# Another step order for four attention mixers, dearer VectorE time in the planner, a two-scalar probability scaling and a last norm that reads PSUM

## The chip, the cores and the metric

One core of one Trainium2 chip runs the whole program. The metric is the device time of one execution in microseconds. Five engines work side by side, each through its own queue in order: TensorE (PE, its weight loads shown apart as PEld), VectorE (DVE), ScalarE (ACT), GpSimd (POOL) and SyncE (SP), which issues most DMAs.

## The reference

Two decoder blocks run one after the other on one sequence of 512 tokens of width 1024, all in float32. The first block is a sparse-attention mixer (compressed, selected and windowed keys, 16 heads), a gated convolutional FFN, a sliding-window mixer with sinks, and a second such FFN. The second block is an "even" mixer (banded attention with sinks beside multi-scale pooling), a squared-ReLU MLP, an "odd" mixer (latent attention beside a bidirectional gated recurrence), and a second MLP. Cut to what matters here:

```python
h = h + mixer(rms_norm(h, g))
h = h + ffn(rms_norm(h, g2))
# inside each attention
p = exp(s - max(s)); p = p / sum(p)      # the scaling of the probabilities
o = p @ v
# at the very end
return rmsnorm(x, final_norm)            # y * rsqrt(mean(y*y) + eps) * g
```

## The kernel before

Activations lie transposed, 128 features by 512 tokens a tile. Every float32 product is made from three products of halves: both operands are split into a rounded high part and a low remainder, so that one projection of a 128-column tile over 1024 features is 24 matmuls of 512 columns. `load` (L866) fetches a weight unit of 512 KB by SP, copies it to the high half (ACT by default) and subtracts to get the low half (DVE by default).

All work is first recorded (`Recorder.add`) and then put in order by `Recorder.order`, a list planner: it walks a simulated time, and at each free engine takes the ready instruction with the lowest number that fits. `Recorder.price` gives each instruction a cost, a latency and a lock (L470 to 506). Some instructions carry alternatives: a copy may go to ACT or DVE (`copy`), a subtraction to DVE or POOL (`tt` with `spare`), a scaling of probabilities (`norm`, L821) to POOL, DVE or ACT. In `best` (L546) the engine that is free compares its wait, its latency and a tax (`TAX`, L355) times its cost with those of the others. The planner's lock rule lets a POOL instruction start at the end of the DVE instruction that holds the lock, and a DVE instruction wait for POOL's.

Within the four mixers the numbers come from hand-written words, `ORDERS` (L359): `play` (L1048) calls one step for each word. `Q`, `K`, `C`, `O` are projections, `a` one tile of scores with its softmax, `p` the transposes of four probability tiles and their product with the values, `L` the reload of one tile of the residual by DMA, `U` one eighth of half of the output projection, and the rest belongs to one mixer each (`c` compression, `G` gates, `T` `D` `E` `S` the recurrence, `P` `M` the pooling). A word's place is a priority. The FFNs and MLPs between the mixers have no words.

The last MLP is made in two halves of 256 columns. `final` (L1847) adds the result to the residual, keeps the sum of squares, multiplies by the gain on ACT, and at the end of a half `after` (L1860) makes the inverse root, spreads it over the partitions by transposes into a PSUM bank, copies that bank to SBUF and multiplies eight tiles by it, on DVE or POOL as the planner chooses, each pair followed by its output DMA. A helper records every operation, so the profile puts all of them on L723.

Of the kernel before, what the change touches and what calls it, by code (L numbers as in the profile page):

```python
# [12 lines left out]
OP = mybir.AluOpType  # L13
# [324 lines left out]
def _width(v):  # L338
# [13 lines left out]
SPILL = {("vector", "gpsimd"): 1.5, ("gpsimd", "vector"): 1.5, ("scalar", "vector"): 2.0, ("scalar", "gpsimd"): 2.0,  # L352
         ("vector", "scalar"): 1.0}
BOOST = 0
TAX = {"gpsimd": 1.0, "vector": 1.0}  # L355
MARGIN = {}
DEEP = 12
DMAQ = 2.0
HORIZON = 3000  # L359
ORDERS = {  # L360
# [26 lines left out]
}  # L387
PATIENCE = 3.0

# [3 lines left out]
class Recorder:  # L393
# [66 lines left out]
    def price(self, eng, name, args, kw, outs, ins):  # L460


        n = max([_width(v) for v in outs + ins if v.idx.size] or [1])
        if name == "dma_start":
            c = 0.48 if any(v.buf.kind == "dram" for v in ins) or not ins else 0.65
            return c, c, ""
        if eng == "tensor":
            lhs, rhs = (args[1], args[2])
            if name == "transpose":
                return 0.109, 0.109, ""  # L470
            w = _width(rhs)
            if lhs.steps and lhs.steps[-1][0] == "bitcast" or lhs.buf.dtype == F32:
                c = max(4 * w / 2400 + 0.0133, 0.214)
            elif lhs.buf.dtype == R32:
                c = max(w / 2400 + 0.0133, 0.112)
            else:
                c = max(w / 2400 + 0.003, 0.056)
            return c, c, ""
        psum = any(v.buf.kind == "bank" for v in ins)
        half = outs[0].shape[0] <= DH if outs else False  # L480
        scalars = sum(isinstance(a, View) and a.shape[1:] == (1,) for a in args[2:] + (kw.get("scalar"),))
        if eng == "scalar":
            w = _width(outs[0])
            c = w / 1200 + (0.055 if psum else 0.11) + 0.18 * isinstance(kw.get("accum_out"), View) + 0.1 * half
            return c, max(c, w / 1200 + (0.175 if psum else 0.205)), ""
        if eng == "vector":
            lock = "D" if n > 64 else ""
            if name == "reciprocal":
                return 0.07, 0.153, ""
            if psum or outs[0].buf.kind == "bank":  # L490
                c, lock = n / 960 + 0.065 + 0.1 * half, ""
            elif name in ("tensor_copy", "memset"):
                c = n / 1920 + 0.075
            elif name == "tensor_scalar":
                c = n / 1920 + 0.065 + 0.07 * scalars
            elif name == "tensor_tensor_scan":
                c = n / 480 + 0.065
            else:
                c = n / 960 + 0.075 + 0.05 * scalars + 0.09 * half
            return c, c + 0.085, lock  # L500
        if name == "tensor_scalar":
            return 0.2 + n / 1100, 0.25 + n / 1100, "p"
        if name == "memset":
            return 0.04 + n / 1100, 0.1 + n / 1100, "p"
        c = (1.0 if OP.pow in kw.values() else 0.05) + n / 445
        return c, c + 0.04, "P"


    def order(self):
# [20 lines left out]
        events, now, result = [0.0], 0.0, []  # L530
        dma_free, table, switched = 0.0, None, -99.0
        slow, window, busy, over = True, 0, 0.0, 0.0
        held = {"D": 0.0, "P": 0.0, "p": 0.0, "": 0.0}

        def arrive(op):
            heapq.heappush(wait[op.eng], (op.ready, op.n, op))
# [8 lines left out]
        def best(op, e):  # L545

            def wait(x):
                lock = cost_on(op, x)[2]
                return max(0.0, held["P"] - now) if lock == "D" else max(0.0, held["D"] - now) if lock else 0.0
            here = wait(e) + cost_on(op, e)[1] + TAX.get(e, 0.0) * cost_on(op, e)[0]  # L550
            for x in (op.eng, *op.alt):
                if x == e:
                    continue
                q = max(0.0, free_at[x] - now)
                for _, _, o in ready[x][:DEEP]:
                    if o is op:
                        break
                    if not o.done and o.eng == x:
                        q += o.cost
                there = max(q, wait(x)) + cost_on(op, x)[1] + TAX.get(x, 0.0) * cost_on(op, x)[0]  # L560
                if there + MARGIN.get((x, e), 0.0) < here:
                    return False
            return True
# [55 lines left out]
        while left:  # L619
# [7 lines left out]
            for e in engines:  # L627
# [7 lines left out]
                while i < min(len(ready[e]) - 1, 200):  # L635
# [43 lines left out]
                    at = now  # L679
                    if op.lock == "D":  # L680
                        at = max(now, now + 0.85 * (held["P"] - now))
                    elif op.lock:
                        at = max(now, held["D"])
                    held[op.lock] = at + cost
                    free_at[e] = at + cost
                    op.end = at + lat
                    if op.fn[0] == "dma_start":
# [54 lines left out]
def _body(tc, ctx, d, out):  # L742
# [76 lines left out]
        nc.vector.tensor_tensor(**kw, alt=[["gpsimd", "tensor_tensor", (), kw]] if spare else None)  # L819

    def norm(o, i, a):  # L821
        nc.gpsimd.tensor_scalar(o, i, a, None, op0=OP.mult, alt=[
            ["vector", "tensor_scalar", (o, i, a, None), {"op0": OP.mult}],
            ["scalar", "activation", (o, i, AF.Copy), {"scale": a}]])

# [106 lines left out]
        nc.gpsimd.tensor_tensor(out=r, in0=ms, in1=e, op=OP.pow)  # L932
        return r

    def spread(r):

        nb = _width(r)
        ps, rb = bank()[:, :nb * P], get()[:, :nb * P]
        for t in range(nb):
            nc.tensor.transpose(ps[:, t * P:(t + 1) * P], r[:, t:t + 1].to_broadcast([P, P]), ident)  # L940
        copy(F(rb), ps)
        return rb

    def norm_out(gains, accs, spill=None):
# [903 lines left out]
    def final(c):  # L1848
# [9 lines left out]
            act(g, hm, scale=pr("fin2")[:, m:m + 1])  # L1858

        def after():  # L1860
            rb = stats(acc)[1]
            for m in range(KT):
                g = gained[m // 2]
                tt(g[:, m % 2], g[:, m % 2], F(rb), OP.mult, True)
                if m >= KT - 2:
                    (nc.sync, nc.scalar)[m % 2].dma_start(out[:, m, c], g[:, m % 2])
                elif m % 2:
# [28 lines left out]
```

## Time and profile before

| | us |
|---|---|
| median of 3 runs | 2329.74 (2329.46 to 2330.76) |
| the profiled execution, whole | 2331.64 |
| its span, first to last instruction | 2329.5 |
| PE busy | 2257.8 (97%) |
| DVE busy | 1719.9 (74%) |
| ACT busy | 968.8 (42%) |
| POOL busy | 242.0 (10%) |
| mean granted clock of TensorE | 0.988 |

The chain of waits shows the stages. The sparse mixer's attention lies from about 75 to 328 us, its FFN to 737, the sliding-window mixer to 847, its FFN to 1290, the even mixer to 1363, its MLP to 1768, the odd mixer to 1932, and the last MLP to about 2318. After that only the last norm is left. The shares of busy time over the whole span mix these stages, and have to be read stage by stage.

### The profile page before, as it was taken

What the parts mean: (1) busy time and instruction counts of PE and PEld (TensorE: products, weight loads), DVE (VectorE), ACT (ScalarE), POOL (GpSimd) and SP (SyncE); (2) the same over time, 40 slices, a digit from 0 to 9 for tenths busy, and PEclk for the clock granted to TensorE, in tenths of its full rate; (3) what the DMA queues carried; (4) which work ended last, traced back from release to release, by engine and by line L of the source; (5) the groups of instructions that cost most, each with busy time, mean ns of one, the idle gap of its engine ahead of it and who ended that gap; (6) DMA issues with size and microseconds to landing.
All of it is one profiled execution on the core that took longest, in us unless ns stands there. A gap on an engine that the chain in (4) does not pass through costs nothing.

```text
span 2329.5 us, 28430 instructions
## 1 busy us (share of the span) xinstructions
PE 2257.8 (97%) x10561; PEld 1844.4 (79%) x10565; DVE 1719.9 (74%) x2792; ACT 968.8 (42%) x1671; POOL 242.0 (10%) x270
## 2 busy tenths in 40 slices
PE   9989999999999999999999999999998889999998
PEld 7767678888888788888888788888886668888888
DVE  7999998858489998758489985444469998444446
ACT  4567863222224864222224652222235775222224
POOL 0211210000001310000001201101102110110111
PEclk9999999999999999999999999999999999999999
DMA  6521112332226313332226222323343112323324
GB/s 213 164 73 46 46 37 91 100 109 93 98 84 192 91 37 100 100 109 92 98 89 192 69 69 98 115 93 100 100 155 121 50 45 64 100 93 98 100 95 132
DMA packets 77243, 230.02 MB, mean 99 GB/s; under 512 B 10288, under 2 KB 12976, under 8 KB 77104
## 3 DMA queue, kind: packets, MB, share of 16 engines
q1 hardware_dynamic: 75584, 226.89, 30.4%
q8 instruction: 83, 1.36, 0.2%
q10 hardware_dynamic: 1520, 1.32, 0.2%
q14 instruction: 56, 0.46, 0.1%
HBM read 206.67 MB, written 8.39 MB: 92 GB/s over the span
## 4 chain that ended last, share of the span: by engine, by line
PE 80%; DVE 12%; ACT 4%; issue 2%; DMA 1%; SPq 1%; POOL 0%; DVEq 0%; ACTq 0%; POOLq 0%
PE bank L723 80%; DVE S L723 7%; ACT S L723 3%; DVE small L723 2%; DVE W L723 2%; DVE D L723 1%; DMA S<-S 1%; SPq L723 1%; ACT W L723 0%; ACT D L723 0%; POOL S L723 0%; DMA D<-D 0%; ACT L723 0%; DMA raw<-in_a_in_dram 0%; DVE bank L723 0%
## 5 line engine op out<-in xcount | busy, mean ns | idle before, releaser
L723 PE MATMUL bank<-S,W 128*128 128x512 f32 (+1 forms) x8028 | 1813.7, 386 | 9.2 <-DVE W L723 5.1
L723 PEld LDWEIGHTS bank<-S,W 128*128 128x128 f32 x8028 | 1476.9, 188 | 308.9 <-DVE W L723 7.9
L723 ACT ACTIVATE W<-raw 128x1024 fp32r<-128x1024 f32 (+2 forms) x368 | 381.3, 1037 | 949.2 <-PE bank L723 843.7
L723 DVE TENSOR_TENSOR W<-raw,W 128x1024 fp32r<-128x1024 f32 (+2 forms) x378 | 501.8, 1328 | 78.2 <-ACT W L723 76.7
L723 DVE TENSOR_TENSOR S<-bank,S 128x512 f32<-128x512 f32 (+5 forms) x412 | 257.2, 634 | 187.9 <-PE bank L723 180.3
L723 DVE TENSOR_TENSOR S<-S,S 128x512 f32<-128x512 f32 (+3 forms) x383 | 267.6, 707 | 14.1 <-ACT S L723 5.3
L723 ACT ACTIVATE S<-S 128x512 fp32r<-128x512 f32 (+2 forms) x219 | 137.0, 629 | 229.4 <-DVE S L723 167.6
L723 DVE TENSOR_TENSOR D<-bank,D 128x512 f32<-128x512 f32 (+2 forms) x113 | 72.6, 651 | 152.0 <-PE bank L723 151.0
L723 DVE SCALAR_TENSOR_TENSOR S<-S,par,S 128x511 f32<-128x511 f32 (+3 forms) x235 | 176.8, 757 | 3.5
L723 PE MATMUL bank<-S,D 128*128 128x512 f32 (+2 forms) x349 | 132.0, 433 | 15.8 <-ACT S L723 7.6
L723 ACT ACTIVATE S<-bank,small 128x512 f32<-128x512 f32 (+6 forms) x247 | 129.1, 531 | 35.7 <-DVE small L723 33.8
L723 DVE SCALAR_TENSOR_TENSOR S<-bank,S 128x512 f32<-128x512 f32 x72 | 49.6, 690 | 123.2 <-PE bank L723 122.1
L723 ACT ACTIVATE S<-bank 128x512 fp32r<-128x512 f32 (+4 forms) x190 | 109.4, 591 | 53.8 <-PE bank L723 47.8
L723 POOL TENSOR_TENSOR S<-S 128x512 f32<-128x512 f32 x66 | 68.9, 1044 | 564.4 <-DVE S L723 544.9
L723 DVE TENSOR_REDUCE small<-bank 128x1 f32<-128x512 f32 (+8 forms) x201 | 120.8, 614 | 8.5 <-PE bank L723 8.0
L723 PE MATMUL bank<-cst,S 128*128 128x128 f32 x716 | 113.8, 278 | 11.8 <-DVE S L723 7.9
L723 PE MATMUL bank<-D,W 128*128 128x512 f32 x480 | 120.9, 395 | 0.2 <-DVE W L723 0.2
L723 POOL TENSOR_TENSOR small<-small,small 128x4 f32<-128x4 f32 (+1 forms) x13 | 13.4, 1031 | 986.5 <-DVE small L723 986.5
L723 PEld LDWEIGHTS bank<-cst,S 128*128 128x128 f32 x716 | 86.9, 143 | 31.1 <-ACT S L723 7.1
L723 PEld LDWEIGHTS bank<-D,W 128*128 128x128 f32 x480 | 88.9, 188 | 18.3 <-DVE W L723 0.6
L723 PEld LDWEIGHTS bank<-S,D 128*128 128x128 f32 x349 | 63.8, 193 | 38.0 <-DVE S L723 15.7
L723 PE MATMUL bank<-S,S 128*128 128x512 f32 (+3 forms) x280 | 73.9, 374 | 14.7 <-ACT S L723 10.8
(114 smaller groups left out, 1176.8 us busy)
## 6 DMA issues: line engine op xcount, KB each, us to landing
raw<-in_f_in_dram SPq DMA_DIRECT2D x88, 512.0 KB, 3.3
raw<-in_m_out_dram SPq DMA_DIRECT2D x72, 512.0 KB, 3.3
raw<-in_m_in_dram SPq DMA_DIRECT2D x64, 512.0 KB, 3.2
raw<-in_f_out_dram SPq DMA_DIRECT2D x32, 512.0 KB, 3.2
raw<-in_a_in_dram SPq DMA_DIRECT2D x17, 512.0 KB, 3.8
raw<-in_o_in_dram SPq DMA_DIRECT2D x15, 512.0 KB, 3.4
S<-S SPq DMA_DIRECT2D x116, 64.0 KB, 2.5
raw<-in_f_out_dram SPq DMA_DIRECT2D x16, 384.0 KB, 3.0
```

The source lines that it names most:

```text
L723: r = getattr(getattr(nc, op.eng), name)(*args, **kw)
```

## The change

It does five things. `TAX` of VectorE goes from 1 to 2, so that the planner gives an instruction with alternatives to DVE only at a shorter queue elsewhere. `price` and the lock rule get other numbers: ACT pays for scale and bias operands that lie in memory, DVE's cheaper scalings cost a little less, rows of odd length more, and a POOL instruction that finds DVE's lock held starts 0.3 of that DVE instruction later. All four `ORDERS` are replaced by other permutations of the same words. The POOL form of `norm` multiplies by the scalar and then by 1.0. In `after` the products of the last norm read the spread inverse root from its PSUM bank on DVE, but for tiles 1 and 3, which POOL makes from the SBUF copy; that copy is put on ACT and feeds POOL alone.

```diff
-TAX = {"gpsimd": 1.0, "vector": 1.0}
+TAX = {"gpsimd": 1.0, "vector": 2.0}
...
-    "nsa": "G Q01 S01 S00 c00 K00 a0312 Q00 S11 S10 K01 a0222 a0310 Q11 c03 c01 c02 a0112 c11 a0010 c12 c10 "
+    "nsa": "Q01 Q00 Q10 K00 S01 G S00 c00 K01 a0310 S11 a0222 c03 a0322 S10 c01 Q30 c02 a0122 c10 a0010 c11 c12 "
...
-    "odd": "C0 G0 R0 V0 O3 T0 K Q0 R1 Q2 C1 k0 Q1 G1 V1 T1 Q3 a00 a02 a03 D0 E0 a01 D1 O2 C2 E1 O0 k2 O1 C3 k4 "
+    "odd": "R0 L4 C0 O3 L1 G0 L5 T0 R1 K V0 Q0 Q3 C1 k0 Q2 G1 L6 Q1 T1 D0 D1 V3 a02 a03 C2 k2 a01 L7 a00 O0 C3 "
...
-            c = w / 1200 + (0.055 if psum else 0.11) + 0.18 * isinstance(kw.get("accum_out"), View) + 0.1 * half
-            return c, max(c, w / 1200 + (0.175 if psum else 0.205)), ""
+            c = _width(outs[0]) / 1200 + (0.055 if psum else 0.11)
+            if isinstance(kw.get("accum_out"), View):
+                return c + 0.18, c + 0.21, ""
+            c += 0.088 * sum(isinstance(kw.get(k), View) for k in ("scale", "bias"))
+            return c + 0.1 * half, c + (0.12 if psum else 0.095), ""
...
-                        at = max(now, held["D"])
+                    elif op.lock and held["D"] > now:
+                        at = held["D"] + 0.3 * held["last"]
...
-        nc.gpsimd.tensor_scalar(o, i, a, None, op0=OP.mult, alt=[
+        nc.gpsimd.tensor_scalar(o, i, a, 1.0, op0=OP.mult, op1=OP.mult, alt=[
...
-            rb = stats(acc)[1]
+            ps, rb = rows_of(rsqrt(acc.mean(1024))), get()[:, :S // 2]
+            nc.scalar.activation(F(rb), ps, AF.Copy)
             for m in range(KT):
                 g = gained[m // 2]
-                tt(g[:, m % 2], g[:, m % 2], F(rb), OP.mult, True)
+                if m in (1, 3):
+                    nc.gpsimd.tensor_tensor(out=g[:, m % 2], in0=g[:, m % 2], in1=F(rb), op=OP.mult)
+                else:
+                    tt(g[:, m % 2], ps, g[:, m % 2], OP.mult)
```

## Rows read from the trace of the kernel before

**Rows 1.** Busy time by engine over the whole span, from the page:
```profile
PE 2257.8 (97%) x10561; PEld 1844.4 (79%) x10565; DVE 1719.9 (74%) x2792; ACT 968.8 (42%) x1671; POOL 242.0 (10%) x270
```

**Rows 2.** Stages: us; busy PE, PEld, DVE, ACT, POOL; granted clock, DMA:
```profile
75.00:328.00 253.00, 228.20 (x1224) 175.58 (x1227) 238.55 (x575) 179.94 (x446) 55.80 (x50) 0.97 0.23 67
328.00:737.00 409.00, 409.00 (x1830) 338.08 (x1829) 308.78 (x436) 117.53 (x143) 3.66 (x5) 1.00 0.33 104
737.00:847.00 110.00, 103.85 (x539) 83.21 (x538) 104.62 (x228) 78.16 (x217) 32.84 (x53) 0.98 0.28 80
...
1290.00:1363.00 73.00, 67.95 (x353) 54.31 (x352) 70.94 (x194) 46.83 (x111) 14.33 (x13) 0.95 0.19 60
...
1768.00:1932.00 164.00, 140.07 (x596) 106.90 (x595) 155.28 (x248) 120.21 (x203) 26.54 (x20) 0.94 0.22 68
...
2317.00:2330.00 13.00, 1.95 (x14) 1.30 (x12) 4.79 (x9) 1.20 (x3) 3.38 (x4) 0.73 0.23 81
```

**Rows 3.** PE's waits, whole span: total us, times, longest:
```profile
PE bank L723 <- ACT S L723: 27.0, 23, 5.3
PE bank L723 <- DVE S L723: 20.2, 22, 3.2
PE bank L723 <- DVE W L723: 6.5, 7, 2.0
PE bank L723 <- DVE D L723: 3.6, 6, 1.3
...
PE bank L723 <- POOL S L723: 0.4, 2, 0.2
```

**Rows 4.** Two 5 us windows of the odd mixer, columns as in the stages:
```profile
1850.00:1855.00 5.00, 3.68 (x9) 2.90 (x10) 5.00 (x7) 2.42 (x3) 0.76 (x2) 0.50 0.01 3
...
1885.00:1890.00 5.00, 0.50 (x1) 0.29 (x1) 4.85 (x7) 4.96 (x9) 0.00 (x0) 0.60 0.39 128
```

**Rows 5.** DVE groups that have alternatives, sparse mixer and odd mixer:
```profile
L723 DVE TENSOR_SCALAR S<-S,small 128x128 f32<-128x128 f32 (+3 forms) x35 | 12.3, 371 | 0.3
L723 DVE CAST S<-bank 128x512 fp32r<-128x512 f32 (+2 forms) x17 | 11.3, 668 | 1.1 <-ACT S L723 0.5 <-DMA S<-S 0.4
L723 DVE COPY S<-bank 128x512 f32<-128x512 f32 (+1 forms) x8 | 5.5, 687 | 0.5 <-PE bank L723 0.4
...
L723 DVE TENSOR_SCALAR S<-S,small 128x512 f32<-128x512 f32 x12 | 5.8, 492 | 0.1
L723 DVE CAST S<-S 128x512 fp32r<-128x512 f32 (+1 forms) x10 | 4.2, 422 | 0.3
```

**Rows 6.** The same work on ACT and on POOL, odd mixer:
```profile
L723 ACT ACTIVATE S<-S,small 128x512 f32<-128x512 f32 x31 | 21.4, 722 | 2.5 <-DVE small L723 2.4
...
L723 POOL TENSOR_SCALAR S<-S,small 128x512 f32<-128x512 f32 x2 | 3.1, 1570 | 39.9 <-DVE small L723 39.9
L723 POOL TENSOR_TENSOR S<-S 128x512 f32<-128x512 f32 x4 | 4.3, 1080 | 31.0 <-PE bank L723 19.6 <-DVE S L723 11.4
```

**Rows 7.** Timeline of the odd mixer around 1848 us:
```profile
1847.62 1.43 POOL L723 TENSOR_TENSOR S<-S,S 128x512 f32<-128x512 f32 x1 [6.23 <-ACT S L723]
1847.95 3.32 DVE L723 TENSOR_TENSOR S<-S,S 128x512 fp32r<-128x512 f32 x2
...
1851.32 1.22 PE L723 MATMUL bank<-S,S 128*128 128x512 f32 x2 [2.83 <-DVE S L723]
...
1858.29 1.29 DVE L723 TENSOR_TENSOR S<-S,S 128x512 fp32r<-128x512 f32 x2
```

**Rows 8.** Timeline of the last norm, to the end:
```profile
2318.15 0.42 DVE L723 TENSOR_TENSOR D<-bank,D 128x256 f32<-128x256 f32 x1 [1.54 <-PE bank L723]
...
2321.53 0.43 PE L723 MATMUL bank<-cst,small 128*128 128x128 f32 x2 [1.50 <-POOL small L723]
2322.00 0.38 ACT L723 ACTIVATE S<-bank 128x256 f32<-128x256 f32 x1 [2.58 <-PE bank L723]
2322.41 3.35 DVE L723 TENSOR_TENSOR S<-S,S 128x256 f32<-128x256 f32 x5 [1.71 <-ACT S L723]
2322.46 2.69 POOL L723 TENSOR_TENSOR S<-S,S 128x256 f32<-128x256 f32 x3 [0.98 <-ACT S L723]
```

More of the change, by code (lines that the diff above doesn't have):

```diff
@@ L482, in price @@
         if eng == "scalar":
-            w = _width(outs[0])
-            c = w / 1200 + (0.055 if psum else 0.11) + 0.18 * isinstance(kw.get("accum_out"), View) + 0.1 * half
-            return c, max(c, w / 1200 + (0.175 if psum else 0.205)), ""
+            c = _width(outs[0]) / 1200 + (0.055 if psum else 0.11)
[3 more added lines that the diff above has]
+            return c + 0.1 * half, c + (0.12 if psum else 0.095), ""
         if eng == "vector":
@@ L489, in price @@
                 return 0.07, 0.153, ""
+            more = 0.0
             if psum or outs[0].buf.kind == "bank":
-                c, lock = n / 960 + 0.065 + 0.1 * half, ""
+                c, lock, more = n / 960 + 0.065, "", 0.1 * half
             elif name in ("tensor_copy", "memset"):
@@ L494, in price @@
             elif name == "tensor_scalar":
-                c = n / 1920 + 0.065 + 0.07 * scalars
+                c = n / 1920 + 0.055 + 0.07 * scalars
             elif name == "tensor_tensor_scan":
@@ L498, in price @@
             else:
-                c = n / 960 + 0.075 + 0.05 * scalars + 0.09 * half
-            return c, c + 0.085, lock
+                c, more = n / 960 + 0.072 + 0.05 * scalars + (0.125 if n % 4 and n > 64 else 0.0), 0.09 * half
+            return c + more, c + 0.085, lock
         if name == "tensor_scalar":
@@ L532, in order @@
         slow, window, busy, over = True, 0, 0.0, 0.0
-        held = {"D": 0.0, "P": 0.0, "p": 0.0, "": 0.0}
+        held = {"D": 0.0, "P": 0.0, "p": 0.0, "": 0.0, "last": 0.0}
         def arrive(op):
@@ L548, in wait @@
                 lock = cost_on(op, x)[2]
-                return max(0.0, held["P"] - now) if lock == "D" else max(0.0, held["D"] - now) if lock else 0.0
+                if lock == "D":
+                    return max(0.0, held["P"] - now)
+                return held["D"] + 0.3 * held["last"] - now if lock and held["D"] > now else 0.0
             here = wait(e) + cost_on(op, e)[1] + TAX.get(e, 0.0) * cost_on(op, e)[0]
@@ L681, in order @@
                         at = max(now, now + 0.85 * (held["P"] - now))
-                    elif op.lock:
-                        at = max(now, held["D"])
+                    elif op.lock and held["D"] > now:
+                        at = held["D"] + 0.3 * held["last"]
                     held[op.lock] = at + cost
+                    if op.lock == "D":
+                        held["last"] = cost
                     free_at[e] = at + cost
@@ L933, in rsqrt, with rows_of, spread @@
         return r
-    def spread(r):
+    def rows_of(r):
         nb = _width(r)
-        ps, rb = bank()[:, :nb * P], get()[:, :nb * P]
+        ps = bank()[:, :nb * P]
         for t in range(nb):
             nc.tensor.transpose(ps[:, t * P:(t + 1) * P], r[:, t:t + 1].to_broadcast([P, P]), ident)
-        copy(F(rb), ps)
+        return ps
+    def spread(r):
+        rb = get()[:, :_width(r) * P]
+        copy(F(rb), rows_of(r))
         return rb
```

48 rows, old and new, of the table ORDERS are left out of this document.

## The prediction

> **What bounds the kernel now.** I read the page's busy times first. PE is busy for 97% of the span [rows 1], so nothing that this change does can matter except where PE is not fully at work, and the next view has to say where that is. The windows by stage show it: in the sparse mixer's FFN PE is busy for all 409 us at full clock, while in the four mixers it stands still for 24.8, 6.2, 5.1 and 23.9 us, the difference of length and PE column, 59.9 us together [rows 2]. The reader is to see two more columns there. DVE is busy for 239 of 253, 105 of 110, 71 of 73 and 155 of 164 us, some 95% of the mixers, against 74% of the whole span [rows 1, 2]: in the mixers PE and DVE are both close to their limit, and each stands still where the order of the work leaves it nothing. And the granted clock falls to 0.97, 0.98, 0.95 and 0.94 [rows 2]. Of its two levels, 1.2 and 2.4 GHz, a window at 0.50 lies wholly at the lower; the rows show such windows where PE was idle for much of the time (at 1850 us 3.7 of 5 busy at 0.50, at 1885 us 0.5 of 5 at 0.60) [rows 4]. One minus the clock, times the length of each mixer, bounds what that costs: 7.6 + 2.2 + 3.7 + 9.8 = 23.3 us. So some 83 us, 3.6% of the time, are open to a better order in the mixers, and 13 us of the last norm to a shorter chain [rows 2].
>
> The third view is that of PE's own waits. DVE ends 20.2 + 6.5 + 3.6 = 30.3 us of them, ACT 27.0 us, POOL 0.4 us [rows 3]. That ACT ends almost as much as DVE, though it is far less busy [rows 2], is the warning in this profile: work that leaves DVE goes to an engine for which PE already waits.
>
> **Dearer DVE time in the planner.** This part can act on instructions with alternatives alone. In the sparse mixer DVE runs 12.3 us of scalings, 11.3 us of high-half copies out of PSUM and 5.5 us of other copies; in the odd mixer 5.8 us of scalings and 4.2 us of high-half copies [rows 5]: 39.1 us. With the doubled tax the planner gives DVE one of these only if ACT's queue is longer than before by one more DVE cost of the instruction. How many move cannot be read from a trace; the ends are none and two thirds, and I take a third, 13 us, because DVE took these in stretches where ACT had a queue as well. A scaling of 512 columns costs 0.72 us on ACT against 0.49 on DVE [rows 5, 6]; copies out of PSUM cost nearly the same. ACT would gain some 16 us, against 73 us that it stands idle in the sparse and 44 in the odd mixer [rows 2]. I count what DVE sheds as PE time only for DVE's part of PE's waits, 30.3 of 57.3, or 0.53: 6.9 us. With less idle time goes part of the clock's loss, in the ratio above, 23.3 to 59.9, or 0.39 for 1: 2.7 us. The sum is 9.6 us, the ends 0 and 19. Where this cover is gone, that is where ACT has no room, the same 16 us stand in front of PE.
>
> **The scaling with two scalars.** POOL's one-scalar form takes 1.57 us for 512 columns [rows 6]. No row shows the two-scalar form. Above, it is bounded by a second pass of the same kind, 3.1 us; below, by the nearest one-input row, the square in place at 1.08 us [rows 6], and a little under that. I take the lower end, since the second factor needs no second stream. PE waited for POOL's tiles for 0.4 us [rows 3], so a shorter scaling gives back 0.4 us at most directly; I take 0.4. If it is longer, its users wait where they didn't: up to 2 us lost. The work that hides it is the rest of the mixer's steps between a score tile and its product.
>
> **Prices, lock rule, new words.** They change no instruction's own duration. They move work. The words of the odd mixer now reload residual tiles (`L`) among the first ten words, so that SP issues these DMAs ahead of later weight loads; DMA is busy for 0.22 of that mixer [rows 2], which hides them. The weight loads of the first projections come before or between them, so I cost that at nothing; a late weight would show as PE waiting for W, 6.5 us now [rows 3]. For the rest, a permutation can close waits or open others, and no row says which. Its value in the sum is nothing; the ends are a third of the 83 us closed (28 us, with the part above) and some 12 us opened (below).
>
> **The last norm.** Now ACT copies the spread root from 2322.00, DVE makes five products from 2322.41 for 3.35 us, to 2325.76, and POOL three in 2.69 us [rows 8]. DVE's 0.67 us for one of them, against 0.42 for a product of the same size that reads PSUM [rows 8], shows that the two engines hold each other up. After the change DVE needs no copy: it starts at about 2322.00 and makes six at 0.42, 2.5 us, to 2324.5. POOL makes two at 0.9 from 2322.46, to 2324.3, which is no later. That saves 1.2 us; what follows (the output DMA) is shifted with it. If DVE's products are still held up, six at 0.67 end at 2326.0, a loss of 0.3. In the first half of the columns the same work lies under PE's.
>
> By the Trainium skill (SBUF — State Buffer, section Who interferes with whom) a VectorE instruction with two SBUF inputs contends with a GpSimd instruction that reads SBUF, and one with at most one SBUF input does not. The trace agrees for the first half: 0.67 against 0.42 us here, and in the odd mixer two subtractions of two SBUF tiles take 3.32 us while POOL works, against 1.29 for two alike [rows 7, 8]. By this rule the tail's saving is 1.2 us; if reading PSUM changed nothing, 0.3 would be lost. I hold with the 1.2.
>
> **Sum.** 9.6 + 0.4 + 1.2 = 11.2 us off the profiled execution's 2331.64 gives 2320.4. That execution lay 1.9 us above the median of the runs, 2329.74, so the forecast for the median is 2318.5, and its own range is 2312 to 2325.
>
> **The rivals.**
> First, the new words close much more than the tax does: a third of the 83 us, 27.7, and 1.2 of the tail, 28.9 us in all, 2301. For it speaks that the waits are many and short, 58 with no more than 5.3 us each [rows 3], which is what an order decides; against it that DVE alone fills 95% of the mixers, so that work must leave it first.
> Second, ACT takes DVE's place. The moved copies and scalings queue on ACT, and PE waits for ACT what it no longer waits for DVE: only 1.6 us remain, 2328. For it speak the 27.0 us, and the window at 1885 us, where ACT and DVE are both full [rows 3, 4].
> Third, the side that would be slower: the tax drives subtractions (`sub`, DVE or POOL) to POOL, where they collide. At 1847.95 us two of DVE's took 3.32 instead of 1.29 us, because POOL ran one of 1.43, and PE waited 2.83 us behind them [rows 7]. If only subtractions move, the 9.6 us are not gained. Each further collision of this kind costs 2.8 us: from three on the kernel is slower by more than 0.2%, and with four it gives 2339. The new lock rule, which prices such a wait higher, speaks against it.
> Last, the change may not do what it says: the words are priorities, and if the planner's choices hardly move, only the tail is left, 2328.5.
>
> **How the numbers follow.** The forecast has 0.50, the order that closes a third 0.17, ACT in DVE's place 0.15, the collisions 0.14, and a plan that hardly moves 0.04. A measurement of this kernel can tell about 0.2%, 4.7 us, from no change. So faster has 0.67, same 0.19, slower 0.14. The range runs from 2302, which leaves out half of the first rival, to 2333, which leaves out most of the collisions.
>
> **What would show it.** In the profile after, DVE's busy time in the mixers should fall by some 13 us, ACT's rise by about as much, and PE's waits for DVE fall by 7 us or more; the four mixers' clock should lie above the present one. POOL's scaling of 512 columns should lie near 1 us. DVE's last six products should take 0.42 us each. If the mixers shorten while DVE's busy time stays, it was the order and not the tax. If PE's waits for ACT grow by what those for DVE lose, the second rival holds; if DVE's subtractions of two SBUF tiles get longer on average, the third.

## The result and the profile after

The changed kernel takes 2300.67 us (median of 4, 2298.52 to 2302.87) against 2329.91: a ratio of 0.9869, interval 0.9857 to 0.9880, or 29 us. The forecast was 2318.5 with a range of 2302 to 2333. The direction was right, the gain was 2.6 times the one forecast, and the time lies just below the range, at that of the first rival.

Busy time by engine over the whole span of after, which answers to [rows 1]:

```profile
PE 2246.6 (98%) x10561; PEld 1840.4 (80%) x10565; DVE 1675.0 (73%) x2697; ACT 984.9 (43%) x1680; POOL 282.2 (12%) x359
```

DVE has 45 us less, ACT 16 us more, POOL 40 us more. The stages can be cut alike in both kernels at POOL's small power instructions, one for each inverse root. These are five of them in the timeline of before (start, us, instruction), and then the same five in after:

```profile
29.76 1.02 POOL L723 TENSOR_TENSOR small<-small,small 128x4 f32<-128x4 f32 x1 [26.83 <-DVE small L723]
...
372.95 1.04 POOL L723 TENSOR_TENSOR small<-small,small 128x4 f32<-128x4 f32 x1 [28.50 <-DVE small L723]
...
1743.05 1.01 POOL L723 TENSOR_TENSOR small<-small,small 128x4 f32<-128x4 f32 x1 [47.21 <-DVE small L723]
...
1972.72 1.04 POOL L723 TENSOR_TENSOR small<-small,small 128x4 f32<-128x4 f32 x1 [46.62 <-DVE small L723]
...
2320.78 0.70 POOL L723 TENSOR_TENSOR small<-small,small 128x2 f32<-128x2 f32 x1 [14.05 <-DVE small L723]
```

```profile
30.52 1.03 POOL L730 TENSOR_TENSOR small<-small,small 128x4 f32<-128x4 f32 x1 [27.31 <-DVE small L730]
...
362.50 1.03 POOL L730 TENSOR_TENSOR small<-small,small 128x4 f32<-128x4 f32 x1 [32.09 <-DVE small L730]
...
1722.52 1.01 POOL L730 TENSOR_TENSOR small<-small,small 128x4 f32<-128x4 f32 x1 [47.20 <-DMA raw<-in_o_in_dram]
...
1946.38 1.03 POOL L730 TENSOR_TENSOR small<-small,small 128x4 f32<-128x4 f32 x1 [6.61 <-DVE small L730]
...
2290.95 0.70 POOL L730 TENSOR_TENSOR small<-small,small 128x2 f32<-128x2 f32 x1 [18.71 <-DVE small L730]
```

The sparse mixer's stage went from 343.2 to 332.0 us, the odd mixer's from 229.7 to 223.9. Cut in the same way, the sliding-window mixer's went from 157.8 to 153.2, the even mixer's from 146.1 to 139.7, the last MLP's, into which the odd mixer's last steps reach, from 348.1 to 344.6, and the time from the last root to the end from 8.7 to 8.1. The two FFNs and the first MLP changed by 1.0 us in sum. The windows of the four mixers, cut there, show why; first before, then after (columns as in [rows 2]):

```profile
29.76:372.95 343.19, 318.37 (x1646) 249.23 (x1649) 316.29 (x702) 220.15 (x505) 64.26 (x57) 0.98 0.26 78
...
734.24:892.06 157.82, 151.67 (x768) 122.72 (x767) 147.04 (x299) 103.37 (x259) 34.97 (x64) 0.99 0.28 83
...
1250.29:1396.42 146.13, 140.97 (x688) 114.15 (x687) 138.20 (x305) 82.49 (x166) 29.22 (x26) 0.98 0.27 83
...
1743.05:1972.72 229.67, 205.74 (x919) 160.67 (x918) 212.44 (x337) 154.78 (x256) 32.25 (x25) 0.96 0.22 69
```

```profile
30.52:362.50 331.98, 312.73 (x1645) 248.53 (x1649) 305.28 (x671) 213.25 (x491) 74.24 (x102) 0.97 0.25 81
...
723.76:876.93 153.17, 148.72 (x763) 120.25 (x762) 142.72 (x292) 100.79 (x254) 38.77 (x76) 1.00 0.25 82
...
1236.31:1376.00 139.69, 138.47 (x689) 112.51 (x688) 131.99 (x291) 83.59 (x168) 38.68 (x38) 1.00 0.27 88
...
1722.52:1946.38 223.86, 207.93 (x934) 162.34 (x933) 207.84 (x327) 152.90 (x245) 54.66 (x49) 0.98 0.21 70
```

PE's idle time in these windows, length minus PE busy, fell from 60.1 to 40.9 us; DVE shed 11.0 + 4.3 + 6.2 + 4.6 = 26.1 us there, ACT shed 10.3 us as well, and POOL took 45.7 us more. The rest of the 28 us by which the four windows shortened is 8.9 us of PE's busy time. So the work of the mixers went to POOL, and not to ACT.

Most of POOL's 46 us are not scalings. Counted over the lines of these windows (SBUF tiles of the two buffer kinds, S and D, together), POOL runs 114 scalings of the probabilities instead of 59, in 71 us instead of 62, and 81 instructions with two SBUF inputs (subtractions, sums and products) instead of 46, in 104 us instead of 67. DVE has 35 fewer of either kind, ACT 20 fewer scalings. The largest group of the second kind on POOL and on DVE over the whole span, before and after:

```profile
L723 POOL TENSOR_TENSOR S<-S,S 128x512 f32<-128x512 f32 (+3 forms) x39 | 62.0, 1600 | 153.8 <-ACT S L723 54.7 <-DVE S L723 41.5 <-issue 37.9
L723 DVE TENSOR_TENSOR S<-S,S 128x512 f32<-128x512 f32 (+3 forms) x383 | 267.6, 707 | 14.1 <-ACT S L723 5.3 <-DMA S<-S 3.3 <-POOL S L723 0.7
```

```profile
L730 POOL TENSOR_TENSOR S<-S,S 128x512 f32<-128x512 f32 (+3 forms) x51 | 72.5, 1426 | 544.1 <-ACT S L730 459.2 <-DVE S L730 49.5 <-DMA S<-S 23.6
L730 DVE TENSOR_TENSOR S<-S,S 128x512 f32<-128x512 f32 (+3 forms) x340 | 237.5, 704 | 16.5 <-POOL S L730 4.0 <-DMA S<-S 3.9 <-ACT S L730 3.2
```

ACT's 16 us more lie outside the mixers: in the two FFNs 36 scalings by a parameter left DVE for ACT, where PE is busy all the time (361.3 of 361.3 us in the first) and nothing is gained by it. PE's waits, one line of before that [rows 3] leaves out, and then after:

```profile
PE bank L723 <- ACT D L723: 0.3, 1, 0.3
```

```profile
PE bank L730 <- DVE S L730: 19.9, 20, 3.2
PE bank L730 <- ACT S L730: 12.0, 13, 3.4
PE bank L730 <- ACT D L730: 4.0, 4, 2.7
PE bank L730 <- DVE D L730: 1.9, 4, 0.8
...
PE bank L730 <- DVE W L730: 1.2, 2, 0.9
```

The waits for ACT's S tiles fell from 27.0 to 12.0 us; with its D tiles (0.3 us before) they fell from 27.3 to 16.0. Those for DVE (S, W and D) fell from 30.3 to 23.0 us, and no line names POOL's S tiles. The scalings of the probabilities in after, over the whole span, by engine, S tiles alone; before had 132 of them on ACT, 72 on DVE (27.9 us) and 57 on POOL (60.5 us) in the same three groups:

```profile
L730 POOL TENSOR_SCALAR S<-S,small 128x512 f32<-128x512 f32 (+3 forms) x110 | 67.1, 615 | 177.9 <-DVE small L730 125.9 <-PE bank L730 32.1 <-ACT S L730 15.7
...
L730 ACT ACTIVATE S<-S,small 128x256 f32<-128x256 f32 (+3 forms) x103 | 56.9, 567 | 20.1 <-DVE small L730 19.3
L730 DVE TENSOR_SCALAR S<-S,small 128x256 f32<-128x256 f32 (+3 forms) x38 | 13.3, 368 | 0.4
```

POOL does nearly twice as many as before in little more time. One of 512 columns takes 0.70 us alone, 384 take 0.59, 256 take 0.48, as three lines of its timeline show. With one scalar they take 1.57 us for 512 [rows 6], and in two lines of the timeline of before, shown first, 0.92 for 256 and 1.56 for 512:

```profile
192.01 0.92 POOL L723 TENSOR_SCALAR S<-S,small 128x256 f32<-128x256 f32 x1 [0.18 <-DVE small L723]
...
205.96 1.56 POOL L723 TENSOR_SCALAR S<-S,small 128x512 f32<-128x512 f32 x1 [3.55 <-DVE small L723]
```

```profile
176.26 0.59 POOL L730 TENSOR_SCALAR S<-S,small 128x384 f32<-128x384 f32 x1 [6.67 <-ACT S L730]
...
177.89 0.70 POOL L730 TENSOR_SCALAR S<-S,small 128x512 f32<-128x512 f32 x1 [0.17 <-DVE small L730]
...
179.94 0.48 POOL L730 TENSOR_SCALAR S<-S,small 128x256 f32<-128x256 f32 x1 [1.36 <-ACT S L730]
```

### The profile page after: what moved, and what is told of

It reads as the page before. It is cut to its first block, busy times and chain, and to the rows that moved or that the text cites. A ratio compares the mean times of both kernels' runs of the same rounds, so it can differ in the third digit from the quotient of the medians.

```text
span 2299.0 us, 28518 instructions
## 1 busy us (share of the span) xinstructions
PE 2246.6 (98%) x10561; PEld 1840.4 (80%) x10565; DVE 1675.0 (73%) x2697; ACT 984.9 (43%) x1680; POOL 282.2 (12%) x359
## 4 chain that ended last, share of the span: by engine, by line
PE 86%; DVE 8%; ACT 3%; issue 1%; DMA 1%; SPq 0%; POOL 0%; DVEq 0%; another core or an unknown queue 0%; ACTq 0%; POOLq 0%
PE bank L730 86%; DVE S L730 4%; ACT S L730 2%; DVE small L730 1%; DVE W L730 1%; DVE D L730 1%; DMA S<-S 1%; SPq L730 0%; DMA D<-D 0%; ACT W L730 0%; ACT D L730 0%; ACT L730 0%; DMA par<-in_params_dram 0%; DMA S<-D 0%; DVE bank L730 0%
## 5 line engine op out<-in xcount | busy, mean ns | idle before, releaser
L730 DVE TENSOR_TENSOR S<-bank,S 128x512 f32<-128x512 f32 (+6 forms) x464 | 285.7, 629 | 252.7 <-PE bank L730 242.5
L730 DVE TENSOR_TENSOR S<-S,S 128x512 f32<-128x512 f32 (+3 forms) x340 | 237.5, 704 | 16.5 <-POOL S L730 4.0
L730 ACT ACTIVATE S<-S 128x512 f32<-128x512 f32 (+3 forms) x223 | 138.5, 623 | 205.1 <-DVE S L730 146.5
L730 DVE SCALAR_TENSOR_TENSOR S<-S,par,S 128x510 f32<-128x510 f32 (+3 forms) x241 | 180.4, 752 | 3.7
L730 POOL TENSOR_TENSOR S<-S,S 128x512 f32<-128x512 f32 (+3 forms) x51 | 72.5, 1426 | 544.1 <-ACT S L730 459.2
L730 ACT ACTIVATE S<-bank,small 128x256 f32<-128x256 f32 (+6 forms) x239 | 124.1, 529 | 30.9 <-DVE small L730 26.6
L730 PE MATMUL bank<-D,W 128*128 128x512 f32 x528 | 134.4, 396 | 0.0
L730 DVE TENSOR_TENSOR D<-bank,D 128x512 f32<-128x512 f32 (+2 forms) x82 | 53.3, 655 | 103.5 <-PE bank L730 103.2
L730 DVE TENSOR_REDUCE small<-bank 128x1 f32<-128x512 f32 (+7 forms) x201 | 120.2, 612 | 9.7 <-PE bank L730 9.2
L730 POOL TENSOR_SCALAR S<-S,small 128x512 f32<-128x512 f32 (+3 forms) x110 | 67.1, 615 | 177.9 <-DVE small L730 125.9
```

The source lines that it names most:

```text
L730: r = getattr(getattr(nc, op.eng), name)(*args, **kw)
```

## The experiments

Three theories stood at the start: the new words bring the gain (A); the quicker POOL scaling does, because the plan relied on it (B); the dearer DVE time does (C). Each run was timed against the kernel before on the same chip.

### One part alone, and one part undone

**The scaling alone**, in the kernel before:

```diff
-        nc.gpsimd.tensor_scalar(o, i, a, None, op0=OP.mult, alt=[
+        nc.gpsimd.tensor_scalar(o, i, a, 1.0, op0=OP.mult, op1=OP.mult, alt=[
```

> The kernel before with one edit: POOL's probability scaling multiplies by the scalar and by 1.0. The order of every engine's instructions is that of before, since the planner's price for this instruction doesn't depend on its operands. Theory A (the new words bring the gain): POOL's tiles cost PE 0.4 us of waits before, so 2329.5, within 1 us of before. Theory B (the plan was right and the chip was not: POOL took 1.57 us for 512 columns where the planner counted 0.67, and every place where the plan relied on it was late): 4 to 10 us faster, 2320 to 2326. Theory C (dearer DVE time): as A.

Measured: 2329.98 us, 0.9991 (0.9982 to 1.0000), 1.5 us less and 4 at most. That is A's and C's number or nearly so, and the lowest edge of B's at best. DVE's and ACT's queues hold the same instructions in the same order as in before, so the run changes this one instruction's time alone.

**The words alone**, in the kernel before: all four entries of `ORDERS` are those of after.

```diff
-    "even": "L6 L0 L2 P0 Q3 K Q1 a113 a003 a103 P3 a022 P1 Q0 a102 L1 Q2 a112 a020 P2 M3 a001 a101 V a021 a110 "
+    "even": "K L2 L4 L7 Q3 Q1 a033 a122 P3 P0 L1 a132 M3 L0 Q2 a101 P1 a120 a110 L5 a022 Q0 a100 a031 a010 a011 "
...
```

> The kernel before with the new words of all four mixers, everything else of before. Theory A: most of the 29 us, 2300 to 2310. Theory B: the words rely on a quick POOL scaling, so without it little, 2320 to 2330. Theory C (the tax moves work off DVE): the words alone bring less than a third, 2320 to 2329.

Measured: 2335.29 us, 1.0017 (1.0007 to 1.0026): 4 us slower than before. A falls; no theory had expected a loss, and all three numbers failed.

**After, with the one-scalar scaling back:**

```diff
-        nc.gpsimd.tensor_scalar(o, i, a, 1.0, op0=OP.mult, op1=OP.mult, alt=[
+        nc.gpsimd.tensor_scalar(o, i, a, None, op0=OP.mult, alt=[
```

> The kernel after with POOL's one-scalar scaling back; the plan is that of after. Some 110 scalings on POOL take about twice as long. Theory A: a few us slower than after, 2301 to 2306. Theory B: most of the gain falls away, 2312 to 2330. Theory C: 2301 to 2306.

Measured: 2312.35 us, 0.9914 (0.9899 to 0.9929), 10 to 12 us slower than after by the ratios and by the times. The queues of DVE and ACT are again those of after. The edit that is worth at most 4 us in the plan of before is worth about 11 in that of after: more than A and C had, and B's number at its lower edge, though without it 19 of the 29 us stay. The groups of scalings on POOL and PE's waits of this run say how: POOL is busy with them for 136 us instead of 67, and PE waits for POOL's S tiles, which it does not in after.

```profile
L730 POOL TENSOR_SCALAR S<-S,small 128x512 f32<-128x512 f32 (+3 forms) x110 | 136.0, 1247 | 141.4 <-DVE small L730 82.3 <-PE bank L730 28.4 <-ACT S L730 14.8
```

```profile
PE bank L730 <- POOL S L730: 8.2, 8, 3.8
```

**After, with prices, lock rule and tax of before:**

```diff
-TAX = {"gpsimd": 1.0, "vector": 2.0}
+TAX = {"gpsimd": 1.0, "vector": 1.0}
...
-            c = _width(outs[0]) / 1200 + (0.055 if psum else 0.11)
+            w = _width(outs[0])
+            c = w / 1200 + (0.055 if psum else 0.11) + 0.18 * isinstance(kw.get("accum_out"), View) + 0.1 * half
...
-                    elif op.lock and held["D"] > now:
-                        at = held["D"] + 0.3 * held["last"]
+                    elif op.lock:
+                        at = max(now, held["D"])
```

> The kernel after with the prices, the lock rule and the tax of before; new words, two-scalar scaling and last norm of after. Theory A: within 6 us of after, 2300 to 2307. Theory B: the same. Theory C: what the tax moves goes back to DVE, at least 10 us slower than after, 2311 to 2325.

Measured: 2331.73 us, 1.0001 (0.9992 to 1.0010). Without the planner's new numbers nothing of the 29 us is left, though the words, the scaling and the last norm are those of after. A and B fall; C had the direction, and the loss is larger than its 2311 to 2325.

### Which of the planner's numbers

C was split: the tax (D), the price formulas (E), or neither by itself, because the words fit this plan and no other (F).

**After, tax back at 1:**

```diff
-TAX = {"gpsimd": 1.0, "vector": 2.0}
+TAX = {"gpsimd": 1.0, "vector": 1.0}
```

> The kernel after with VectorE's tax back at 1; new words, prices, lock rule, scaling and last norm stay. Theory D (the new words and the tax are worth something only together, and the tax is what sends scalings to POOL): most of the gain goes, 2318 to 2332. Theory E (the corrected prices are what the words need): within 5 us of after, 2300 to 2306.

Measured: 2346.42 us, 1.0066 (1.0051 to 1.0081), beyond what any theory had expected.

**After, with the price formulas of ACT and DVE of before**, tax and lock rule of after:

```diff
-            c = _width(outs[0]) / 1200 + (0.055 if psum else 0.11)
+            w = _width(outs[0])
+            c = w / 1200 + (0.055 if psum else 0.11) + 0.18 * isinstance(kw.get("accum_out"), View) + 0.1 * half
...
```

> The kernel after with the price formulas of ACT and DVE of before; tax 2, new lock rule, words, scaling and last norm of after. Theory D: within 6 us of after, 2300 to 2307. Theory E: 2315 to 2332. Theory F (the words fit one plan and no other, so that any edit of the plan loses most of it): 2315 to 2332 here and with the old tax and with the old lock rule.

Measured: 2337.55 us, 1.0031 (1.0019 to 1.0044).

**After, with price formulas and lock rule of before**, tax of after:

```diff
...
-                    elif op.lock and held["D"] > now:
-                        at = held["D"] + 0.3 * held["last"]
+                    elif op.lock:
+                        at = max(now, held["D"])
```

> The kernel after with the price formulas and the lock rule of before; tax 2, words, scaling and last norm of after. Theory D: 2300 to 2310. Theory E: 2315 to 2332. Theory F: 2315 to 2332.

Measured: 2334.48 us, 1.0012 (1.0002 to 1.0021).

**After, with the words of before in three mixers** (`swa`, `even`, `odd`):

```diff
-    "swa": "L6 Q5 K L7 a212 Q4 a202 Q1 a232 Q3 Q2 Q0 a120 a022 a100 Q7 L5 a012 a032 a230 a030 Q6 a002 a010 a110 "
+    "swa": "Q5 Q3 K Q1 a202 Q4 Q2 a112 Q0 a100 a030 a020 a122 a022 Q7 a110 L7 a130 a032 Q6 a002 a010 a102 a000 "
...
```

> The kernel after with the words of before in the sliding-window, even and odd mixers; the sparse mixer keeps its new words. Theory D: those three gave back 20 us between the roots that mark their stages; the tax alone, on the old words, keeps a third to a half of it, 2310 to 2315. Theory E: 2303 to 2310. Theory F (tax and prices bring nothing to words that weren't chosen with them): 2320 or more.

Measured: 2331.48 us, 1.0001 (0.9992 to 1.0010).

All four runs lost the whole gain, as F alone had it. F's number itself came in the last run only: the first three lie 14, 5.5 and 2.5 us above its 2332, which is 3 to 15 us slower than the kernel before. D failed in all four. E failed in the first and the last, and in the two between it had the same number as F. The stages, cut at the roots of each profiled run:

| us | sparse | sliding window | even | odd | last MLP | last root to end |
|---|---|---|---|---|---|---|
| before | 343.2 | 157.8 | 146.1 | 229.7 | 348.1 | 8.72 |
| after | 332.0 | 153.2 | 139.7 | 223.9 | 344.6 | 8.05 |
| scaling alone | 339.5 | 157.4 | 145.8 | 231.2 | 348.1 | 9.14 |
| words alone | 336.3 | 166.3 | 143.9 | 235.1 | 345.2 | 8.72 |
| after, one scalar | 334.0 | 153.2 | 141.5 | 232.4 | 344.6 | 7.74 |
| after, prices, lock and tax of before | 335.8 | 164.9 | 145.0 | 234.5 | 345.2 | 7.75 |
| after, tax 1 | 350.6 | 162.6 | 145.4 | 238.1 | 345.8 | 7.93 |
| after, old formulas | 333.9 | 159.4 | 145.0 | 248.2 | 345.2 | 7.74 |
| after, old formulas and lock | 341.4 | 162.6 | 146.2 | 234.9 | 345.2 | 7.96 |
| after, old words in three | 332.3 | 165.4 | 149.3 | 231.8 | 348.1 | 7.72 |

The sliding-window, even and odd mixers reach their best times only where new words meet the new plan. In the last row the sparse mixer, which has both, keeps its 332, while the sliding-window and even mixers, with old words and new plan, are slower than in either kernel. For the sparse mixer the rule is weaker: the new words alone take 7 of its 11 us, and it is nearly as fast with the old formulas (333.9), but slowest of all with tax 1 (350.6).

### How narrow the fit is, and what the plan is worth with words of its own

**After, with two neighbouring words of the sparse mixer swapped:**

```diff
-           "a0321 a0212 a0311 Q21 c13 a0312 C a0020 B0 a0313 Q20 p0310 Q11 a1211 a1120 a0211 a0213 a0110 a0323 "
+           "a0212 a0321 a0311 Q21 c13 a0312 C a0020 B0 a0313 Q20 p0310 Q11 a1211 a1120 a0211 a0213 a0110 a0323 "
```

> The kernel after with one edit: in the words of the sparse mixer two neighbours, two score tiles of the first head group, a0321 and a0212, change places. Prices, tax, lock rule, scaling and last norm stay, and no instruction's work changes. Theory F (the gain is the fit of just these words to just this plan): 5 to 15 us slower than after, 2306 to 2316, part of it in stages far behind the swap. Theory D (a plan with tax and new prices is good for any sensible words): within 2 us of after, 2299 to 2303.

Measured: 2306.06 us, 0.9893 (0.9877 to 0.9910), 5 to 6 us above after; the two intervals overlap by 0.0003, so this is likely and not certain. The roots put the loss at the far end: sparse mixer 332.0 us, unchanged, but odd mixer 227.3 and last MLP 346.5, 3.5 and 1.9 us more than in after. Compared instruction by instruction, DVE's and ACT's queues of the two kernels differ in the sparse mixer, are the same in the five stages behind it, and differ again in the odd mixer, whose words are the same. The planner carries something across the stages in between; what that is was not tested.

**Tax 1 with words of its own.** The words were searched for this plan, starting from those of after, in which single words were moved and a move was kept if it shortened the planner's own sum.

```diff
-TAX = {"gpsimd": 1.0, "vector": 2.0}
+TAX = {"gpsimd": 1.0, "vector": 1.0}
...
-    "nsa": "Q01 Q00 Q10 K00 S01 G S00 c00 K01 a0310 S11 a0222 c03 a0322 S10 c01 Q30 c02 a0122 c10 a0010 c11 c12 "
+    "nsa": "Q00 Q01 Q10 K00 S01 S00 G c00 K01 a0310 S11 a0222 a0322 c03 S10 c01 a0010 Q30 c02 c10 a0122 c11 c12 "
...
```

> The kernel after with VectorE's tax at 1 and with words of its own: they were searched for this plan, by moving single words and keeping what shortens the planner's own sum, starting from those of after, for as long as those of the next kernel. Theory F1 (words fitted to their plan recover what a plan can give; the tax is then worth what remains): far faster than with the words of after (2346), but no better than before, 2322 to 2334. Theory F2 (any plan does as well as any other once its words fit it, so the tax is worth nothing): the same as the next kernel, within 5 us.

Measured: 2331.93 us, 1.0000 (0.9991 to 1.0010).

**Tax 2 with words of its own**, searched in the same way and for as long, from the words of before in three mixers (the kernel of 2331 us above).

```diff
-    "swa": "L6 Q5 K L7 a212 Q4 a202 Q1 a232 Q3 Q2 Q0 a120 a022 a100 Q7 L5 a012 a032 a230 a030 Q6 a002 a010 a110 "
...
+    "swa": "K Q5 Q3 Q1 a202 Q4 Q2 a112 Q0 a100 a030 a020 a122 a022 Q7 a110 a130 L7 a032 Q6 a002 a010 a102 a000 "
...
```

> The kernel after, tax 2, with words searched in the same way and for as long, starting from those of before in the sliding-window, even and odd mixers (2331 with these). Theory F1: 12 to 22 us faster than the kernel before it in this call, 2308 to 2316. Theory F2: within 5 us of it.

Measured: 2318.54 us, 0.9949 (0.9933 to 0.9966).

Words of their own took 14 us off the first plan and 13 off the second, so a plan gives back something once its words are fitted to it, and the plan with tax 2 ends 13 us the faster, as F1 has it (its 2308 to 2316 was missed by 2.5 us). But the two searches did not start alike. In the sparse mixer both started from the words of after, which go with tax 2, and there lie 8.9 us of the difference, 331.7 against 340.6 us; the sliding-window mixer has 3.9 of it, the even and odd mixers 1.5 and 0.4. What tax 2 is worth when both plans have words equally well fitted is not shown. In the groups of scalings, tax 1 first, the plans differ as after differs from before:

```profile
L730 ACT ACTIVATE S<-S,small 128x512 f32<-128x512 f32 (+3 forms) x130 | 74.3, 593 | 20.8 <-DVE small L730 20.2
L730 POOL TENSOR_SCALAR S<-S,small 128x256 f32<-128x256 f32 (+3 forms) x58 | 33.3, 574 | 232.7 <-DVE small L730 117.4 <-PE bank L730 51.1 <-issue 34.6
...
L730 DVE TENSOR_SCALAR S<-S,small 128x256 f32<-128x256 f32 (+3 forms) x61 | 22.6, 381 | 0.4
```

```profile
L730 POOL TENSOR_SCALAR S<-S,small 128x256 f32<-128x256 f32 (+3 forms) x116 | 68.6, 595 | 223.3 <-DVE small L730 157.6 <-PE bank L730 20.9 <-ACT S L730 19.4
...
L730 ACT ACTIVATE S<-S,small 128x512 f32<-128x512 f32 (+3 forms) x99 | 55.6, 575 | 16.5 <-DVE small L730 16.0
L730 DVE TENSOR_SCALAR S<-S,small 128x256 f32<-128x256 f32 (+3 forms) x40 | 14.0, 367 | 0.7
```

### The last norm

The timeline of after, from the spreading of the last root, answers to [rows 8]:

```profile
2291.70 0.69 PE L730 MATMUL bank<-cst,small 128*128 128x128 f32 x2 [1.49 <-POOL small L730]
2292.42 0.38 ACT L730 ACTIVATE S<-bank 128x256 f32<-128x256 f32 x1 [2.83 <-PE bank L730]
2292.84 2.08 DVE L730 TENSOR_TENSOR S<-bank,S 128x256 f32<-128x256 f32 x6 [1.97 <-ACT S L730]
2292.88 1.41 POOL L730 TENSOR_TENSOR S<-S,S 128x256 f32<-128x256 f32 x2 [1.24 <-ACT S L730]
```

The six products alone, in groups (busy, mean of one):

```profile
L730 DVE TENSOR_TENSOR S<-bank,S 128x256 f32<-128x256 f32 x6 | 2.1, 413 | 2.0 <-ACT S L730 2.0
```

DVE's six products read PSUM, but begin only when ACT has copied that bank.

```diff
-            nc.scalar.activation(F(rb), ps, AF.Copy)
             for m in range(KT):
...
                     tt(g[:, m % 2], ps, g[:, m % 2], OP.mult)
+                if m == 0:
+                    nc.scalar.activation(F(rb), ps, AF.Copy)
```

> The kernel after, but in the last norm DVE's first product is recorded ahead of ACT's copy of the same PSUM bank. In after DVE's six products begin 0.04 us after the end of that copy, though they don't read it. If the wait is there because two engines' readings of one bank are put in the order in which they are recorded, DVE starts some 0.4 us sooner and the copy comes behind its first product: the time from the last inverse root to the end is 7.4 to 7.7 instead of 8.05 us. If it is not that, DVE's start stays where it was.

Measured: one run, 2299.63 us. Its timeline:

```profile
2289.63 0.70 POOL L730 TENSOR_TENSOR small<-small,small 128x2 f32<-128x2 f32 x1 [18.71 <-DVE small L730]
...
2290.38 0.43 PE L730 MATMUL bank<-cst,small 128*128 128x128 f32 x2 [1.50 <-POOL small L730]
2290.85 0.42 DVE L730 TENSOR_TENSOR S<-bank,S 128x256 f32<-128x256 f32 x1 [1.30 <-PE bank L730]
2291.31 0.39 ACT L730 ACTIVATE S<-bank 128x256 f32<-128x256 f32 x1 [3.04 <-DVE S L730]
2291.73 1.75 DVE L730 TENSOR_TENSOR S<-bank,S 128x256 f32<-128x256 f32 x5 [0.45 <-ACT S L730]
```

The order turned round with the record: DVE's first product, then ACT's copy, then DVE's other five, each 0.03 to 0.04 us after the end of the one before. In both runs the readers of this bank followed each other in recorded order; what makes the second one wait was not tested. The expected gain did not come: 8.2 us from the root to the end instead of 8.1. Up to the last product it is 3.85 us instead of 3.97, but there after is not the run to compare with: its two transposes took 0.69 us at a granted clock of 0.50, those of this run 0.43 at 1.00. The run with one scalar has the last norm of after and quick transposes:

```profile
2302.56 0.70 POOL L730 TENSOR_TENSOR small<-small,small 128x2 f32<-128x2 f32 x1 [18.71 <-DVE small L730]
2303.31 0.43 PE L730 MATMUL bank<-cst,small 128*128 128x128 f32 x2 [1.50 <-POOL small L730]
...
2304.20 2.08 DVE L730 TENSOR_TENSOR S<-bank,S 128x256 f32<-128x256 f32 x6 [1.72 <-ACT S L730]
```

There the last product ends 3.72 us after the root, and 3.71 or 3.72 in the four other runs with this norm and quick transposes. So the edit let DVE begin 0.42 us sooner and made it stand 0.46 us between its first and its second product; in this one run it cost 0.1 us.

## Why the prediction was wrong

**What bounds the kernel: right.** All of the gain lies in the four mixers, what runs over from them, and the last norm; the PE-bound stages did not move. PE's idle time fell, its waits for DVE by 7.3 us (forecast: 7 or more), and the clock rose from 0.988 to 0.992; it rose in three mixers, and fell from 0.98 to 0.97 in the sparse one.

**The step that failed is the sum itself.** It priced the parts one by one, gave the new words nothing ("no row says which"), the tax 9.6 us and the scaling 0.4, and added them. The runs show that these parts have no price of their own: the words alone lose 4 us, the words with scaling and last norm but the old planner numbers give 0, the pieces of the planner put back give 2331 to 2346, the scaling is worth at most 4 us in one plan and 10 to 12 in the other. What the change brings is a plan together with words fitted to it. I should have read the words in the diff as chosen under the other edits of the same diff, and have set the pair against the 83 us that were open, instead of taking an average permutation for it. How the words were found is not shown; the runs show that they fit these numbers and none of the other sets that were tried.

**The first rival had the right time and a wrong reason.** Its 2301 us came from a third of the 83 us, a share that no row gave, so that its time was met by luck. It had the words close the waits by themselves; alone they close 7 us in the sparse mixer and open 8.5 and 5.4 in the sliding-window and odd ones.

**Where DVE's work goes: wrong.** I had it on ACT, at 13 us in the mixers. DVE shed 26 us there, and ACT did too, 10 us; POOL took it. I had fixed on ACT because POOL's scaling stood at 1.57 us [rows 6], although the same diff was to change that. And I had counted scalings and copies alone: 35 instructions with two SBUF inputs moved as well, which carry 37 of POOL's 46 us, and DVE's copies out of PSUM did not leave it (61 in the mixers instead of 53).

**The two-scalar scaling: its size was wrong.** I took 1.08 us "and a little under" for 512 columns; it is 0.70. The planner's own price for it stands in the kernel before, 0.2 + 512/1100 = 0.67 us, and was nearer. From 256 to 512 columns it costs 0.86 ns a column where the one-scalar form costs 2.5 (0.92 us to 1.56 in the trace of before). The Trainium skill (GPSIMD Engine Reference, section 3.1) gives 1.03 cycles per element for a body of at most two operations; worked out at that page's 1.2 GHz, this is an estimate of 0.86 ns. The two-scalar form agrees with its 0.86 ns, the one-scalar form with its 2.5 does not. And the bound of 0.4 us on its worth came from PE's waits for POOL under the plan of before, which say nothing about a plan that gives POOL twice as many scalings.

**The last norm: the number right, by two errors that cancel.** Forecast 1.2 us. With transposes as quick as in before, the last product ends 3.72 us after the root (the run with one scalar) instead of 4.98, 1.26 us less; in after itself, with its slower transposes, it ends 3.97 us after the root, and the end comes 0.7 us earlier (8.05 against 8.72). DVE started with the end of ACT's copy, 0.4 us later than I had it. And each of its six products took 0.41 us, as I had it, but in the trace they overlap, so that the six took 2.08 us and not 2.5.

**The other rivals did not come, though the third's condition did.** ACT did not take DVE's place. The planner did move instructions with two SBUF inputs to POOL, but they collided no more dearly than before: DVE's largest such group beside the weight loads takes 704 ns on average (340 instructions) against 707 (383). One small group got longer, 92 products with the gates, from 14.2 to 18.7 us.

## What to carry to other kernels

When a planner's numbers and a hand-ordered input that was fitted to them change in one diff, price them as one thing: here neither half alone said anything about the pair, and the room that is open in the stage is a better bound than a sum of the parts. A change that makes an idle engine's instruction cheaper can be worth little in the old plan and more in a plan that uses it: at most 4 us and about 11 here. An order of this kind is narrow: the old tax, the old price formulas, old words in three mixers or the slow scaling each cost about 10 us or more, and two neighbouring steps swapped likely 5, so it is worth fitting again after an edit of a price.

## What the runs showed that was not expected

POOL's multiplication by a scalar takes about half as long with a second scalar factor of 1.0 as without it: 0.70 against 1.57 us for 512 columns, 0.48 against 0.92 for 256. And swapping two steps of the first mixer left that mixer's time alone and lengthened the odd mixer, some 1,600 us later, by 3.5 us.
